# Softmax over rows of 512: interleaving loads and stores in one DMA queue

## The chip, the cores and the metric

The kernel runs on one core of a Trainium2 chip. The metric is the time of one execution on the device, in microseconds. The engines named here are TensorE (PE, not used for arithmetic in this kernel), VectorE (DVE), ScalarE (ACT), GpSimd (POOL) and SyncE (SP), which only issues transfers. "held" is the buffer on the chip; "DRAM" is the memory off the core, where the input and the output lie.

## The reference

The input x has 16 x 1024 x 512 values of float32, so 16384 rows of 512. Each row is replaced by its softmax:

```python
x_max = np.max(x, axis=-1, keepdims=True)
exp_x = np.exp(x - x_max)
return (exp_x / np.sum(exp_x, axis=-1, keepdims=True)).astype(np.float32)
```

33.55 MB are read and 33.55 MB are written.

## The kernel before

**Tiles.** 128 partitions each hold 128 rows. The rows of a partition are counted 0 to 127 and cut into 16 groups of 8 (GROUP), and into 8 blocks of 16 (BLOCKS), so a block is two groups. A block is 128 partitions x 16 rows x 2 KB, 4 MB in all, and is one transfer: one load from x or one store to out. The text calls the loads L0 to L7 and the stores S0 to S7; block n holds groups 2n and 2n+1.

**The buffer.** held has room for 96 rows per partition (RING), so for six blocks. Blocks 0 to 5 have rows of their own. Block 6 uses the rows of block 0 again and block 7 those of block 1, so L6 may start only when S0 has landed, and L7 only when S1 has.

**The work on a group.** DVE takes the negated maximum of each row (step M, L164). ACT runs eight activations, one for each row slot, that write the exponential in place and add up the row's sum (L195); it goes through the groups 0 to 15 in order. DVE takes the reciprocal of the sums (L170). Then the group is multiplied by it in place (L172): on POOL for groups 0 to 11 (step P), on DVE for groups 12 to 15 (step V). The order of DVE's steps is written out by hand in VECTOR: it begins M0 M1 P0 M2 P1 M3 and goes on with M8 P6 M9 P7 and so forth, and ends with

```python
P10 M12 P11 M13 V12 M14 V13 M15 V14 V15
```

Here a P step is the reciprocal on DVE, which releases POOL's multiplication, so DVE's wait for M12's load stands ahead of the reciprocal of group 11.

**The order of transfers.** All transfers are issued by SP, on one hardware queue, in the order of the list ORDER. The first AHEAD entries, all of them loads, are issued without a wait at the start of the program (the first even ahead of the program's start barrier, in loads_at_the_head). The rest follows in a loop: ahead of a load SP waits for the stores that free its rows (semaphore stored), ahead of a store it waits for the scaling of the store's two groups (semaphores scaled):

```python
for what, k in ORDER[AHEAD:]:
    if what == "L":
        ...
        load(k)
    else:
        ...
        nc.sync.dma_start(out=in_dram(out_rows, *k), in_=rows(*k)).then_inc(
```

SP runs its list strictly in order: while it waits for one entry, the next ones stand behind it. Each load has a semaphore of its own that the M step of its first group waits for; at the end SP waits for the stores that no load has waited for. The load's issue is at L126, the store's at L152, and all waits of an engine's queue are at L110.

In the kernel before, ORDER is six loads, three stores, two loads, five stores.

Of the kernel before, what the change touches and what calls it, by code (L numbers as in the profile page):

```python
# [1 line left out]

# [4 lines left out]

F32 = mybir.dt.float32
EXP = mybir.ActivationFunctionType.Exp
AX = mybir.AxisListType.X  # L10

GROUP = 8
GROUPS = 16
RING = 12 * GROUP

BLOCKS = [(0, 16), (16, 32), (32, 48), (48, 64), (64, 80), (80, 96), (96, 112), (112, 128)]
ORDER = [
    ("L", (0, 16)),
    ("L", (16, 32)),
    ("L", (32, 48)),
    ("L", (48, 64)),
    ("L", (64, 80)),
    ("L", (80, 96)),
    ("S", (0, 16)),
    ("S", (16, 32)),  # L30
    ("S", (32, 48)),
    ("L", (96, 112)),
    ("L", (112, 128)),
    ("S", (48, 64)),
    ("S", (64, 80)),
    ("S", (80, 96)),
    ("S", (96, 112)),
    ("S", (112, 128)),
]
AHEAD = 6  # L40

VECTOR = """
    M0 M1 P0 M2 P1 M3 P2 M4 P3 M5 P4 M6 P5 M7 P6 M8 P7 M9 P8 M10 P9 M11
    P10 M12 P11 M13 V12 M14 V13 M15 V14 V15
"""

AT_HEAD = {mybir.EngineType.SP: 1}

def loads_at_the_head(nc):

    main, body = nc.main_func.blocks[0], nc.main_func.blocks[1]
    for engine, count in AT_HEAD.items():
        loads = [
            i
            for i in body.instructions
            if i.engine == engine and type(i).__name__ == "InstDMACopy"  # L60
        ][:count]
        barrier = next(
            n
            for n, i in enumerate(main.instructions)
            if i.engine == engine and type(i).__name__ == "InstDrain"
        )
        for load in loads:
            body.instructions.remove(load)
        main.instructions[barrier:barrier] = loads


@with_exitstack
def kernel(
    ctx: ExitStack,
    tc: tile.TileContext,
    x: bass.AP,
    out: bass.AP,
):
    nc = tc.nc
    nc.at_finalize(loads_at_the_head)  # L80
    P = nc.NUM_PARTITIONS

    d = x.shape[-1]
    x_rows, out_rows = x.flatten_outer_dims(), out.flatten_outer_dims()
    assert x_rows.shape[0] == GROUPS * GROUP * P

    def in_dram(rows, a, b):

        first, last = next(k for k in BLOCKS if k[0] <= a and b <= k[1])
        block = rows[first * P : last * P].rearrange("(p r) d -> p r d", p=P)  # L90
        return block[:, a - first : b - first, :]

    held = nc.alloc_sbuf_tensor("held", [P, RING, d], F32).ap()
    shift = nc.alloc_sbuf_tensor("shift", [P, GROUPS * GROUP], F32).ap()
    sums = nc.alloc_sbuf_tensor("sums", [P, GROUPS * GROUP], F32).ap()
    recip = nc.alloc_sbuf_tensor("recip", [P, GROUPS * GROUP], F32).ap()

    loads = [k for what, k in ORDER if what == "L"]
    stores = [k for what, k in ORDER if what == "S"]
    loaded = {k: nc.alloc_semaphore(f"loaded{k[0]}") for k in loads}  # L100
    scaled = [nc.alloc_semaphore(f"scaled{g}") for g in range(GROUPS)]
    stored = {k: nc.alloc_semaphore(f"stored{k[0]}") for k in stores}
    maxed = nc.alloc_semaphore("maxed")
    expd = nc.alloc_semaphore("expd")
    to_pool = nc.alloc_semaphore("to_pool")
    to_vector = nc.alloc_semaphore("to_vector")

    def take(engine, semaphore, n):

        engine.wait_ge(semaphore, n).then_inc(semaphore, -n)  # L110

    def rows(a, b):
        assert a // RING == (b - 1) // RING
        return held[:, a % RING : (b - 1) % RING + 1, :]

    def meets(k, a, b):
        return k[0] < b and a < k[1]

    def group(g):
        return g * GROUP, (g + 1) * GROUP  # L120

    def stats(t, g):
        return t[:, g * GROUP : (g + 1) * GROUP]

    def load(k):
        copy = nc.sync.dma_start(out=rows(*k), in_=in_dram(x_rows, *k))  # L126
        copy.then_inc(loaded[k], 16)
        return copy

    with tc.manual_schedule():
        for _, k in ORDER[:AHEAD]:
            tc.no_tile_sem_insts.add(load(k).ins.name)
    tc.close()
    tc.compile()  # L137

    taken, done = set(), set()
    for what, k in ORDER[AHEAD:]:  # L140
        if what == "L":
            for s in stores:
                if meets(s, k[0] - RING, k[1] - RING) and s not in taken:
                    take(nc.sync, stored[s], 16)
                    taken.add(s)
            load(k)
        else:
            for g in range(GROUPS):
                if meets(k, *group(g)) and g not in done:
                    take(nc.sync, scaled[g], 1)  # L150
                    done.add(g)
            nc.sync.dma_start(out=in_dram(out_rows, *k), in_=rows(*k)).then_inc(  # L152
                stored[k], 16
            )


    seen = set()

    def rowmax(g):
        for k in loads:  # L160
            if meets(k, *group(g)) and k not in seen:
                take(nc.vector, loaded[k], 16)
                seen.add(k)
        nc.vector.reduce_max(  # L164
            out=stats(shift, g), in_=rows(*group(g)), axis=AX, negate=True
        ).then_inc(maxed, 1)

    def scale(g, engine, ready):
        take(nc.vector, expd, 1)
        nc.vector.reciprocal(out=stats(recip, g), in_=stats(sums, g)).then_inc(ready, 1)  # L170
        take(engine, ready, 1)
        engine.tensor_mul(  # L172
            out=rows(*group(g)),
            in0=rows(*group(g)),
            in1=stats(recip, g).unsqueeze(2).to_broadcast([P, GROUP, d]),
        ).then_inc(scaled[g], 1)

    for step in VECTOR.split():
        what, g = step[0], int(step[1:])
        if what == "M":  # L180
            rowmax(g)
        elif what == "V":
            scale(g, nc.vector, to_vector)
        else:
            scale(g, nc.gpsimd, to_pool)


    nc.scalar.preload_act_table(EXP)  # L188

    with nc.scalar.Fori(0, GROUPS) as i:  # L190
        take(nc.scalar, maxed, 1)
        for r in range(GROUP):
            row = held[:, bass.ds(i % (RING // GROUP) * GROUP + r, 1), :]
            at = bass.ds(i * GROUP + r, 1)
            act = nc.scalar.activation(  # L195
                out=row,
                in_=row,
                func=EXP,
                bias=shift[:, at],
                scale=1.0,  # L200
                accum_out=sums[:, at],
            )
        act.then_inc(expd, 1)


    for k in stores:
        if k not in taken:
            take(nc.sync, stored[k], 16)


# [1 line left out]
_INS = ['x']  # L212
_OUTS = [((16, 1024, 512), 'float32')]


# [23 lines left out]
```

## Time and profile before

| What | Value |
|---|---|
| Median of 3 runs | 160.15 us (160.12 to 160.21) |
| Profiled execution | 160.14 us, of which the span shown is 158.8 us |
| DVE, ACT, POOL busy | 90.6, 92.0 and 84.0 us |
| DMA queue busy | 98.9% of 16 engines' span, 67.11 MB |
| One maximum of a group on DVE (L164) | 4399 ns, 16 of them |
| One exponential on ACT (L195) | 712 ns, 128 of them |
| One scaling on POOL and on DVE (L172) | 7015 ns and 4570 ns |

The busy shares say how long an engine worked in the whole span. The waits say for what an engine stood still. For transfers two numbers are read together: when SP issued one (its start in the timeline), and how long it took from issue to landing; the sum is when the data had arrived. A transfer that is issued while others are still in the queue has their time in its own.

### The profile page before, as it was taken

Reading aid. Unit: us, or ns where it says so; the run is one execution under the profiler, and the core shown is the slowest. Engines: PE = TensorE matmul, PEld = TensorE weight load, DVE = VectorE, ACT = ScalarE, POOL = GpSimd, SP = SyncE. Lnnn points to the kernel's source line nnn. Section 1 sums busy time; section 2 is a strip of 40 time slices with the busy share of each in tenths; the row PEclk is TensorE's granted clock in tenths of the full one; section 3 lists DMA queues with packets and bytes.
Section 4 is the critical chain, followed back from the end, with each engine's and each line's share of the span. In section 5 each row is a group of like instructions: output and inputs, shape, how many; then the busy total and the mean of one; then the engine's idle time right before and its main releaser. Section 6 shows DMA issues by size and latency. Waiting matters only on the chain. (4 is left out here: it accounts for less than half of the span.)

```text
span 158.8 us, 747 instructions
## 1 busy us (share of the span) xinstructions
DVE 90.6 (57%) x36; ACT 92.0 (58%) x257; POOL 84.0 (53%) x16
## 2 busy tenths in 40 slices
DVE  0008959777977977887700000795999998640000
ACT  0300699999999999999993000059934929200000
POOL 0000009999999999999999999259200000000000
DMA  7999999999999998999999999999999999999996
GB/s 264 470 454 396 413 487 421 396 454 470 396 396 487 437 396 380 413 396 454 470 396 421 462 437 396 446 479 396 421 446 454 396 437 473 413 404 454 446 413 264
DMA packets 2305, 67.12 MB, mean 423 GB/s; under 512 B 256, under 2 KB 256, under 8 KB 256
## 3 DMA queue, kind: packets, MB, share of 16 engines
q1 hardware_dynamic: 2304, 67.11, 98.9%
q14 instruction: 1, 0.01, 0.0%
HBM read 33.55 MB, written 33.55 MB: 423 GB/s over the span
## 5 line engine op out<-in xcount | busy, mean ns | idle before, releaser
L195 ACT ACTIVATE held<-held,shift x128 | 90.3, 712 | 40.0 <-ACTq L110 40.0
L172 POOL TENSOR_TENSOR held<-held,recip 128x4096 f32<-128x4096 f32 x12 | 83.8, 7015 | 28.0 <-POOLq L110 28.0
L164 DVE TENSOR_REDUCE shift<-held 128x8 f32<-128x4096 f32 x16 | 70.3, 4399 | 33.2 <-DVEq L110 33.2
L195 ACT ACTIVATION_READ_ACCUMULATOR held<-held,shift x128 | 24.6, 192 | 0.0
L172 DVE TENSOR_TENSOR held<-held,recip 128x4096 f32<-128x4096 f32 x4 | 18.3, 4570 | 0.6
L170 DVE RECIPROCAL recip<-sums 128x8 f32<-128x8 f32 x16 | 3.2, 201 | 16.5 <-DVEq L110 16.5
L188 ACT ACT_TABLE_LOAD x1 | 1.3, 1283 | 3.9 <-PEq L137 3.9
L223 POOL MEMSET const-float32-0.0<- 128x1 f32 x1 | 0.1, 98 | 0.2 <-issue 0.2
L223 POOL MEMSET const-uint8-127<- 128x1 uint8 x1 | 0.1, 102 | 0.0
L223 POOL MEMSET const-bfloat16-1.0<- 128x1 bf16 x1 | 0.1, 101 | 0.0
L223 POOL MEMSET const-float32-1.0<- 128x1 f32 x1 | 0.1, 98 | 0.0
## 6 DMA issues: line engine op xcount, KB each, us to landing
held<-in_x_dram SPq DMA_DIRECT2D x8, 4096.0 KB, 29.7
out_dram<-held SPq DMA_DIRECT2D x8, 4096.0 KB, 28.3
```

The lines of the kernel that those rows point to most:

```text
L164: nc.vector.reduce_max(out=stats(shift, g), in_=rows(*group(g)), axis=AX, negate=True).then_inc(maxed, 1)
L170: nc.vector.reciprocal(out=stats(recip, g), in_=stats(sums, g)).then_inc(ready, 1)
L172: engine.tensor_mul(out=rows(*group(g)), in0=rows(*group(g)), in1=stats(recip, g).unsqueeze(2).to_broadcast([P, GROUP, d]),).then_inc(scal ...
L188: nc.scalar.preload_act_table(EXP)
L195: act = nc.scalar.activation(out=row, in_=row, func=EXP, bias=shift[:, at], scale=1.0, accum_out=sums[:, at],)
L223: nc = _bacc.Bacc("TRN2", target_bir_lowering=False, num_devices=1)
```

## The change

The list ORDER is rewritten and AHEAD goes from 6 to 5. Afterwards SP issues five loads, then S0, L5, S1, L6, S2, L7, and then S3 to S7. Nothing else is edited. In the built program the instructions of DVE, ACT and POOL stand in the same order as before; only SP's list differs. On it, the wait for S0's landing (for L6) now stands ahead of the wait for groups 4 and 5 (for S2), and L5 stands behind the wait for groups 0 and 1 (for S0).

```diff
     ("L", (32, 48)),
     ("L", (48, 64)),
     ("L", (64, 80)),
+    ("S", (0, 16)),
     ("L", (80, 96)),
-    ("S", (0, 16)),
     ("S", (16, 32)),
+    ("L", (96, 112)),
     ("S", (32, 48)),
-    ("L", (96, 112)),
     ("L", (112, 128)),
     ("S", (48, 64)),
     ("S", (64, 80)),
@@ -37,7 +37,7 @@
     ("S", (96, 112)),
     ("S", (112, 128)),
 ]
-AHEAD = 6
+AHEAD = 5
```

## The prediction

> **What bounds the kernel now.** I read the page first: busy times, slices, DMA queues, chain. Columns in the first two parts: busy us and share of the span, then tenths and GB/s in 40 slices of 3.97 us.
>
> ```profile
> DVE 90.6 (57%) x36; ACT 92.0 (58%) x257; POOL 84.0 (53%) x16
> ...
> DMA  7999999999999998999999999999999999999996
> GB/s 264 470 454 396 413 487 421 396 454 470 396 396 487 437 396 380 413 396 454 470 396 421 462 437 396 446 479 396 421 446 454 396 437 473 413 404 454 446 413 264
> ...
> q1 hardware_dynamic: 2304, 67.11, 98.9%
> HBM read 33.55 MB, written 33.55 MB: 423 GB/s over the span
> ...
> DVE held L172 3%
> ```
>
> No compute engine is over 58% busy, while the one DMA queue works for 98.9% of the span and has no empty slice. The chain of waits reaches back only to the last scale (3% of the span): after it comes one long transfer that the chain does not follow.
>
> Next, where each transfer ends. The timeline gives an issue's start (first column), and the DMA view, narrowed to that issue, the time to landing (last column). The fifth load, the sixth, the first store and the last store:
>
> ```profile
> 2.16 0.44 SPq L126 DMA_DIRECT2D held<-in_x_dram  x1
> 2.65 0.49 SPq L126 DMA_DIRECT2D held<-in_x_dram  x1
> 37.54 0.35 SPq L152 DMA_DIRECT2D out_dram<-held  x1
> 140.91 0.33 SPq L152 DMA_DIRECT2D out_dram<-held  x1
> ```
>
> ```profile
> held<-in_x_dram SPq DMA_DIRECT2D x1, 4096.0 KB, 48.9
> held<-in_x_dram SPq DMA_DIRECT2D x1, 4096.0 KB, 58.8
> out_dram<-held SPq DMA_DIRECT2D x1, 4096.0 KB, 33.6
> out_dram<-held SPq DMA_DIRECT2D x1, 4096.0 KB, 17.9
> ```
>
> Issue plus time to landing: the fifth load (call it L4, counting from 0) lands at 2.16 + 48.9 = 51.1, L5 at 61.5, store S0 at 71.1, S7 at 158.8, which is the span's end. The same sum for the others gives L0 12.2, L1 21.9, L2 31.6, L3 41.3; S1 80.9, S2 90.8, L6 100.3, L7 110.1; S3 119.8, S4 129.6, S5 139.4, S6 149.1. So transfers land one by one in the order of issue, 9.7 to 9.8 us apart whether they load or store. Only L5, the last before the first turn from loads to stores, takes 10.4: 0.7 more. The turn from stores to loads (S2 to L6: 9.5, rounded) and the second turn from loads to stores (L7 to S3: 9.7) show nothing.
>
> Last, what the compute engines wait for:
>
> ```profile
> 68.27 4.42 DVE L164 TENSOR_REDUCE shift<-held 128x8 f32<-128x4096 f32 x1
> 73.89 4.37 DVE L164 TENSOR_REDUCE shift<-held 128x8 f32<-128x4096 f32 x1
> 79.41 0.20 DVE L170 RECIPROCAL recip<-sums 128x8 f32<-128x8 f32 x1 [1.16 <-DVEq L110]
> 100.45 4.42 DVE L164 TENSOR_REDUCE shift<-held 128x8 f32<-128x4096 f32 x1 [20.83 <-DVEq L110]
> 136.38 4.43 DVE L172 TENSOR_TENSOR held<-held,recip 128x4096 f32<-128x4096 f32 x1
> ```
>
> The maxima M10 and M11 (first two lines) use L5 about 7 us after it landed. M12 stands still for 20.83 us until L6 lands at 100.3. The last scale ends at 140.8, but S6 holds the queue until 149.1, so even the last store waits 8.2 us behind other transfers.
>
> **The change, part by part.** The bytes, the sixteen transfers, their sizes and all compute instructions stay; only SP's list changes. New queue order: L0 to L4, S0 L5 S1 L6 S2 L7, S3 to S7.
>
> *Five loads at the head instead of six.* L0 to L4 are issued and land as before, the last at 51.1. S0 is issued when POOL has scaled groups 0 and 1, as now at 37.5, which is 13.6 us before the queue would run dry (now 24). L5 needs no store to have landed (it takes free rows), so it follows S0 at about 37.9. One issue of 0.49 us leaves the head; nothing waits for it, since the DVE's first work waits for L0 at 12.2.
>
> *S0 ahead of L5.* They exchange places: S0 lands near 61.5, L5 at 71.1, together the same 20.0 us that the two take now. L5 is 9.6 us later, and M10 goes from 68.27 to about 71.3: 3 us late on the DVE. ACT finishes exp 9 at 73.8 and then waits for M10 until 75.7; exps 10 and 11 (8 rows at 0.705, 5.64 us each) end at 81.3 and 87. POOL runs P0 to P10 without a break to 100.2 (P9 at 86.2, P10 at 93.2). Recip 9, behind M10, is done by 75.9, recip 10 by 81.5: 10 and 11 us of cover. Without this cover each further us would pass to S4 and S5, which still have over 20 us of slack below.
>
> *S1 ahead of L6, L6 ahead of S2.* S1 is issued at 51.5 as now (its groups), while the queue is full until 71.1. L6 needs S0's rows: SP waits for S0's landing and issues L6 at 61.6 instead of 71.28. Behind this wait in SP's queue stands S2, whose groups are ready at 65.4, so it loses nothing. L6 lands at 90.8, 9.5 earlier; S2 at 100.3.
>
> *L7 behind S2.* It needs S1, and SP waits till 80.9, as now (80.96). Behind it stands S3, ready at 79.5 by POOL and issued at about 81.4; now 81.48. L7 lands at 110.1, as now.
>
> *What follows.* M12 starts at 90.9 rather than 100.45 and the DVE's 20.83 us hole mostly closes. P11 starts at 100.2 instead of 105.16 and ends at 107.2: S5 at 107.3 (112.27 now). V12 runs from about 101.3; in the trace its kind took 5.00 us where it shared 0.7 us with a POOL scale, otherwise 4.43. Now it lies wholly beside P11. Lower bound 5.0, upper bound: it waits for P11's end, 107.2 + 4.4 = 111.6. I take the upper one. Then M14 (L7 landed at 110.1) ends at 116.0, and V13, M15, V14, V15, each with a 0.2 us reciprocal and short gaps, at 120.8, 125.2, 129.9 and 135.5. S6 is issued at 120.9 (125.56 now), S7 at 135.6 (140.91).
>
> *The sum.* The queue is filled until, at each issue: S1 71.1 (20 ahead), L6 80.9 (19), S2 90.8 (25), L7 100.3 (19), S3 110.1 (29), S4 at 93.3 119.8 (26), S5 129.6 (22), S6 139.4 (18), S7 149.1 (13). Thus no transfer is ever awaited by the queue; the earlier compute of 5 us buys slack for S7 and no time. The end stays at 12.2 + 15 places x 9.73 + 0.7 of one turn = 158.8. The profiled execution took 160.14 with a span of 158.8, so 1.3 us lie outside; the median before is 160.15. Forecast: 160.15.
>
> *The unknown: turns.* The order has three changes of direction now and seven afterwards; from load to store two now, four afterwards. One turn, the first, shows 0.7 us; the two others show none within the rounding. Bounds for the four added turns: 0 and 4 x 0.7 = 2.8; below nothing at most the 0.7 itself. I take 0, by the nearest rows, the later turns, which like the new ones stand in a queue already writing; the first turn stays, in another place.
>
> The Trainium skill, "DMA: Bandwidth & Descriptors", section "Anatomy of one DMA — SWDGE (gpsimd) path", gives a DMA a nearly constant cost of about 2.0 us, mostly the confirmation of the last written bytes; paid again at four added turns that would be +8, an estimate from that page. By the trace here it is not paid between queued transfers: 9.7 us apart, whatever the direction.
>
> **The rivals.**
>
> *Slower: every turn from load to store stalls the queue.* Place: the last packets of a load before a store. Price: 0.7 per turn, as at L5. Two turns are added: 160.15 + 1.4 = 161.5; with only one of them, 160.8. It decides from 0.16 us a turn (two make the 0.32 of the bound below). For: L5's landing. Against: L7 to S3, 9.7. Chance 0.20. That all four turns cost 0.7 (162.9): 0.03.
>
> *Slower: a full drain at each turn.* As a mechanism of this kernel it is the queue standing empty between two directions; a load alone at the head shows that: L0 lands 12.2 after issue instead of 9.7, so 2.5 a turn and 4 x 2.5 = 10: 170. Against: three turns in the trace at 0.7 or less. Chance 0.02. The skill's fixed cost named above is such a rule.
>
> *Slower: the later L5 becomes the bound.* It would need S4 over 26 us late; chance 0.02, 161 or more.
>
> *Faster: the 0.7 belongs to six loads in a row, not to the first store.* Then five loads escape it: 160.15 - 0.7 = 159.45. For: the excess is in a load's time, and L0 to L4 have none. Against: it comes right at the first store. More is hardly to be had: the other places are at 9.7 already, and loads and stores take the same, so mixing has nothing to overlap. Chance 0.15.
>
> *Not doing what it says:* the built order of SP is the one described, so no chance for that.
>
> **The numbers.** Runs of before lie within 0.1 us; a difference of 0.2% (0.32 us) is about what a measurement of this kernel can tell from no change. No change 0.58; slower 0.20 + 0.03 + 0.02 + 0.02 = 0.27; faster 0.15. The range takes in the loss of the one stall below, 159.4, and two turns above, 161.6; it leaves out about 1 in 10. The likeliest case alone spans 159.9 to 160.4.
>
> **What would show it.** Right: the DMA row full in every slice at 98.9%; landings near 61.5 (S0), 71.1 (L5), 90.8 (L6), 110.1 (L7), 158.8 (S7); M10 near 71.3, M12 near 90.9, the last scale ending near 135, S7 landing over 20 us after its issue. Wrong: places of more than 9.8 us at S0, S1, S2 or S3 (a price per turn); a landing of S0 9.7 after L4 (the stall is gone); a slice of the DMA row below 9 in the middle (starved queue); or a scale that ends after the store ahead of it has landed.

## The result and the profile after

The kernel after takes 160.78 us in the median of 13 runs (160.28 to 162.16), the kernel before 160.12 in 13 runs beside them. The ratio is 1.0042, 95% interval 1.0026 to 1.0058: slower by 0.67 us (0.42 to 0.93). Its runs also lie further apart than those of before (160.05 to 161.10). The profiled execution took 160.39 us with a span of 159.1, so it shows a little over a third of the loss (160.39 against 160.14). No slower run of after has a trace; what the rest of the loss consists of is inferred from the traces of the other kernels below.

The page of after, busy times, slices and queue:

```profile
DVE 94.8 (60%) x36; ACT 92.1 (58%) x257; POOL 83.9 (53%) x16
...
DMA  7999999999999999999999999999999999999996
GB/s 264 478 445 396 437 486 396 396 478 445 396 445 346 396 445 461 412 396 461 461 396 420 445 445 404 445 461 404 429 437 445 414 429 437 445 420 437 453 412 264
...
q1 hardware_dynamic: 2304, 67.11, 98.9%
```

The queue is still full from end to end, with the same 98.9%. Apart from the two ends, the lowest slice, 346 GB/s, is now the 13th (47.7 to 51.7 us), where L4 turns into S0; in before the dip (380) was the 16th, at L5 and S0. Nothing ran dry, yet the same bytes took longer.

The timeline of SP and the DMA view of after for L4, S0, L5, L6 and S7 (issue first, time to landing last):

```profile
2.18 0.44 SPq L126 DMA_DIRECT2D held<-in_x_dram  x1
37.45 0.35 SPq L152 DMA_DIRECT2D out_dram<-held  x1
37.85 0.43 SPq L126 DMA_DIRECT2D held<-in_x_dram  x1
61.92 0.33 SPq L126 DMA_DIRECT2D held<-in_x_dram  x1
135.83 0.33 SPq L152 DMA_DIRECT2D out_dram<-held  x1
```

```profile
held<-in_x_dram SPq DMA_DIRECT2D x1, 4096.0 KB, 49.7
out_dram<-held SPq DMA_DIRECT2D x1, 4096.0 KB, 24.4
held<-in_x_dram SPq DMA_DIRECT2D x1, 4096.0 KB, 33.5
held<-in_x_dram SPq DMA_DIRECT2D x1, 4096.0 KB, 29.1
out_dram<-held SPq DMA_DIRECT2D x1, 4096.0 KB, 23.2
```

L4 lands at 51.9 (51.1 before), S0 at 61.9, L5 at 71.4, L6 at 91.0, S7 at 159.0. S7 stands 23.2 us in the queue. The compute engines have no part in the end. DVE's timeline of after, M10, M12, V12 and V15:

```profile
71.52 4.42 DVE L164 TENSOR_REDUCE shift<-held 128x8 f32<-128x4096 f32 x1 [3.27 <-DVEq L110]
91.12 4.42 DVE L164 TENSOR_REDUCE shift<-held 128x8 f32<-128x4096 f32 x1 [8.73 <-DVEq L110]
102.12 9.25 DVE L172 TENSOR_TENSOR held<-held,recip 128x4096 f32<-128x4096 f32 x1
131.31 4.42 DVE L172 TENSOR_TENSOR held<-held,recip 128x4096 f32<-128x4096 f32 x1
```

M10 is 3.3 us late and M12 9.3 us early, as worked out; the last scale ends at 135.7.

**Where the time is.** A transfer is cut into 128 packets of 32 KB, eight for each of 16 DMA engines. The trace has a record of each packet, and about nine in ten of them, loads and stores alike, take 1213 ns. The records do not name the engine; the packets fall into 16 chains, as each starts within a few ns of another's end, and a chain is taken for an engine. What a packet takes beyond 1213 ns (beyond 611 ns, for one of 16 KB) is called excess here. Summed over an engine's packets and averaged over the 16 engines, for the two profiled executions:

```
                                        before   after
start of L0                              0.64    0.59 us
load ahead of the first store (L5, L4)   0.90    0.99
after only: L5 ahead of S1                -      0.08
after only: L6 ahead of S2                -      0.09
L7 ahead of S3                           0.01    0.09
everything else                          0.07    0.07
mean excess of an engine                 1.62    1.91
the slowest engine's end behind the mean 0.49    0.61
```

The later excess sits in the last packet or two of a load that is followed by a store; no store that is followed by a load has it. The mean engine loses 0.29 us more. The slowest engine, which alone ends the last store, is 0.12 further behind the mean, but this difference by itself shows nothing: in traces of other kernels with the two turns of before it is 0.49 to 0.78 behind (E1 0.78, E3 0.75, E7 0.49), and in before it comes from a single halt of one engine in S5 (0.30 us without a packet, and the next one 0.38 us longer). In after it comes from the turns: the engine that ends last is 0.27 us behind the mean when L4 ends, 0.36 after L5, 0.48 after L6, 0.67 after L7, and hardly moves during the stores (0.61 at the end).

### The profile page after: what moved, and what is told of

Same layout as the page of the kernel before. It is cut to its first block, busy times and chain, and to the rows that moved or that the text cites. A ratio compares the mean times of both kernels' runs of the same rounds, so it can differ in the third digit from the quotient of the medians.

```text
span 159.1 us, 747 instructions
## 1 busy us (share of the span) xinstructions
DVE 94.8 (60%) x36; ACT 92.1 (58%) x257; POOL 83.9 (53%) x16
## 3 DMA queue, kind: packets, MB, share of 16 engines
q1 hardware_dynamic: 2304, 67.11, 98.9%
## 5 line engine op out<-in xcount | busy, mean ns | idle before, releaser
L195 ACT ACTIVATION_READ_ACCUMULATOR held<-held,shift x128 | 24.0, 187 | 0.0
L172 DVE TENSOR_TENSOR held<-held,recip 128x4096 f32<-128x4096 f32 x4 | 22.5, 5632 | 0.6
```

The costliest lines, as they stand in the source:

```text
L172: engine.tensor_mul(out=rows(*group(g)), in0=rows(*group(g)), in1=stats(recip, g).unsqueeze(2).to_broadcast([P, GROUP, d]),).then_inc(scal ...
L195: act = nc.scalar.activation(out=row, in_=row, func=EXP, bias=shift[:, at], scale=1.0, accum_out=sums[:, at],)
```

## The experiments

Theory A is that each turn from load to store costs time in the DMA engines; B, that five loads instead of six ahead of the first store do. Changes in us are the ratio to before, in runs beside each other, times 160.15, with the 95% interval. The ratio is not that of the two medians; where they tell different things, both are given.

**E1, the head alone.** Edit: `-AHEAD = 6` to `+AHEAD = 5`, the order of before kept.

> The order of before, but only five loads issued at the head (AHEAD 5); L5 is then issued a little later, still without a wait, and still ahead of S0. Theory A (each load followed by a store costs time at the turn; two turns here as before): 160.1. Theory B (what costs is that five instead of six loads run ahead of the first store): 160.1, since the queue's order is unchanged. If the later issue of L5 itself were the cause: about 160.8, as after.

Measured: 160.24, ratio 0.9996 (0.9986 to 1.0005). The later issue of L5 costs nothing.

**E2, one more turn.**

```diff
     ("L", (64, 80)),
+    ("S", (0, 16)),
     ("L", (80, 96)),
-    ("S", (0, 16)),
     ("S", (16, 32)),
...
-AHEAD = 6
+AHEAD = 5
```

> Five loads, S0, L5, S1, S2, L6, L7, then the five last stores: three turns from load to store, one more than before. Theory A: after added two turns and 0.66 us, so a third of a us each: 160.45. Theory B (five loads ahead of the first store): all of it, 160.8.

Measured: 160.42, ratio 1.0019 (1.0002 to 1.0036), so +0.30 (0.03 to 0.58); the medians differ by 0.16. The added turn, L5 to S1, has a mean excess of 0.10 us, and up to 0.39 on one engine.

**E3, five loads, but two turns as before.**

```diff
     ("L", (64, 80)),
-    ("L", (80, 96)),
     ("S", (0, 16)),
     ("S", (16, 32)),
     ("S", (32, 48)),
+    ("L", (80, 96)),
     ("L", (96, 112)),
...
-AHEAD = 6
+AHEAD = 5
```

> Five loads, S0 S1 S2, L5 L6 L7, then the five last stores: two turns from load to store, as before, but five loads at the head. L5 lands near 91, so M10 is late; by the trace's durations the last scale still ends near 142, ahead of the queue. Theory A: 160.1. Theory B: 160.8.

Measured: 160.31, ratio 1.0004 (0.9995 to 1.0012). Theory B falls: five loads ahead of the first store cost nothing while the turns stay at two.

**E4, five turns.** ORDER is L0 to L3, S0 L4 S1 L5 S2 L6 S3 L7, S4 to S7, and AHEAD 4.

> Four loads, then S0 L4 S1 L5 S2 L6 S3 L7, then the four last stores: five turns from load to store, three more than before. Theory A: 160.1 + 3 x 0.33 = 161.1. Theory B (the shorter the run of loads ahead of the first store, the more): two fewer loads, 161.4; the two differ in e3, here only a price below 160.5 would speak against both.

Measured: 162.08, ratio 1.0106 (1.0071 to 1.0141), so +1.70 (1.14 to 2.26), more than three times a third of a us and more than either theory said. By issue plus time to landing, the loads L4 to L7 ahead of a store take 10.0, 10.0, 10.1 and 10.2 us from the landing before them, and the stores 9.7. The end of the queue shows how that comes about. The windows view (length, busy time of DVE, ACT and POOL, clock, DMA share, GB/s of the packets that start in the window), first before, then this kernel:

```profile
157.00:157.50 0.50, 0.00 (x0) 0.00 (x0) 0.00 (x0) 1.00 0.31 131
157.50:158.00 0.50, 0.00 (x0) 0.00 (x0) 0.00 (x0) 1.00 0.01 0
158.00:158.50 0.50, 0.00 (x0) 0.00 (x0) 0.00 (x0) 1.00 0.00 0
```

```profile
157.00:157.50 0.50, 0.00 (x0) 0.00 (x0) 0.00 (x0) 1.00 0.46 197
157.50:158.00 0.50, 0.00 (x0) 0.00 (x0) 0.00 (x0) 1.00 0.16 66
158.00:158.50 0.50, 0.00 (x0) 0.00 (x0) 0.00 (x0) 1.00 0.31 131
```

131 GB/s for 0.5 us are two packets of 32 KB. Before, the last two engines start their last packet before 157.5; here three packets start after that, two of them after 158, while the other engines have nothing left to do. The mean engine ends only 0.10 us later than in before (157.91 against 157.82); the slowest, at 159.57, is 1.66 behind the mean instead of 0.49. It was 0.61 behind when L3 ended, then 0.68, 0.88, 1.31 and 1.72 after L4, L5, L6 and L7.

**E5 and E6, a small store early.** Edit on before and on after, AHEAD 2 in both; not shown: POOL fills the tile warm with zeros at the start, and SP waits for warm_done ahead of S0.

```diff
     ("L", (16, 32)),
+    ("W", None),
     ("L", (32, 48)),
...
+        elif what == "W":
+            take(nc.sync, warmed, 1)
+            nc.sync.dma_start(
+                out=in_dram(out_rows, 127, 128)[:, :, 0:128], in_=warm
+            ).then_inc(warm_done, 16)
```

> The order of before with one small extra store (128 x 512 bytes of zeros into rows of out that S7 writes over later) behind L1, so that a store has gone out long before S0. Theory F (the stall of about 0.9 us at the end of L5 is paid once, at the first store of the program): the stall moves to L1 or vanishes, and the packets of L5 show none; 160.1 if it moves, 159.3 if a small store pays less. Theory T (a stall at the turn after a long run of loads, whatever was stored before): L5 shows its 0.9 again, and the extra turn adds 0.1 to 0.9: 160.3 to 161.1.

> The order of after with the same small extra store behind L1. Theory F: L4 shows no stall, the later turns keep their small ones: 160.0 to 160.8. Theory T: L4 shows 0.9 again, 160.9 to 161.7.

Measured: 160.34 (ratio 1.0004, 0.9992 to 1.0016) and 160.68 (1.0022, 1.0002 to 1.0042). The stall ahead of S0 is still there, 0.85 us on L5 and 0.86 on L4, so a small store ahead does not pay it; theory F falls for a store of 64 KB. The time of E6 lies below the 160.9 that theory T said. The store itself takes 0.19 us of the queue and its turn shows no more than that. The two kernels differ by 0.34 in the medians, half of what before and after differ by.

**E7 and E8, before and after without most of the arithmetic.**

```diff
-            out=stats(shift, g), in_=rows(*group(g)), axis=AX, negate=True
+            out=stats(shift, g), in_=rows(*group(g))[:, :, 0:16], axis=AX, negate=True
...
-            row = held[:, bass.ds(i % (RING // GROUP) * GROUP + r, 1), :]
+            row = held[:, bass.ds(i % (RING // GROUP) * GROUP + r, 1), 0:16]
```

and so for the scale.

> The order of before; maxima, exponentials and scales work on 16 of the 512 columns only (most of the arithmetic is left out), the transfers are whole. The DMA queue is full either way. Theory A (turns cost in the DMA engines themselves): 160.1, with a 0.9 us stall at L5. Rival C (what costs at the turns is the compute engines' traffic on held): the stall is gone, 159.2.

> The order of after with the same thin compute. Theory A: 160.8, so 0.66 above e7. Rival C, or a cause in the later L5 or in the scales that stand beside each other: the same as e7 within 0.1.

The pages of the two, busy times and DMA row:

```profile
DVE 7.3 (5%) x36; ACT 39.3 (25%) x257; POOL 5.0 (3%) x16
...
DMA  7999999999999998999999999999999999999996
```

```profile
DVE 7.3 (5%) x36; ACT 39.3 (25%) x257; POOL 5.0 (3%) x16
...
DMA  7999999999999999999999999999999999999994
```

Measured: 160.03 (ratio 0.9985, 0.9973 to 0.9996) and 160.65 (1.0031, 1.0016 to 1.0046). With DVE at 5% and POOL at 3% the order of after still costs 0.62 us in the medians, and the first stall is there too (0.86 and 0.91). Rival C falls; the later M10 and the scale that stands beside another have no part in it. E7 itself is 0.24 us below before (0.06 to 0.43); its trace does not show why (mean excess 1.59 against 1.62).

**E9, six loads at the head and one turn added late.**

```diff
     ("L", (96, 112)),
+    ("S", (48, 64)),
     ("L", (112, 128)),
-    ("S", (48, 64)),
     ("S", (64, 80)),
```

> The order of before with six loads at the head, and S3 moved between L6 and L7: three turns from load to store instead of two, nothing else. Theory A (a turn after a single load costs 0.1 to 0.3 us, partly by putting the 16 engines further out of step): 160.3 to 160.5, with an excess on the last packets of L6 and L7 before the stores. Theory B (the head of five loads): 160.1. By the trace's durations the last scale ends near 146, still ahead of S7's place at 149; if that failed, the queue would show a gap ahead of S7.

Measured: 160.37, ratio 1.0035 (1.0005 to 1.0064), so +0.56 (0.08 to 1.02). Three of its twelve runs, from 161.81 to 162.21, carry most of this; the medians differ by 0.18, and one of the 24 runs of before beside it took 161.81 too. DVE's last scale and the DMA row of this kernel:

```profile
140.44 4.42 DVE L172 TENSOR_TENSOR held<-held,recip 128x4096 f32<-128x4096 f32 x1
```

```profile
DMA  7999999999999999999999999999999999999994
```

The scale ends at 144.9, ahead of S7's place, and no slice is short of work until the last. L6 ahead of S3 has a mean excess of 0.07 and L7 ahead of S4 0.16; the stall of 0.86 at L5 is that of before. So a turn costs with six loads at the head as well, though this run shows it barely clear of the noise.

**E10 and E11, halved transfers, few turns and many.** Edit: BLOCKS of 8 rows. E10 (AHEAD 12): L0 to L11, S0 to S5, L12 to L15, S6 to S15. E11 (AHEAD 10): L0 to L9, then S0 L10 S1 L11 to S5 L15, then S6 to S15.

> All transfers halved (16 loads and 16 stores of 2 MB, 8 rows per partition), in the order of before: twelve loads, six stores, four loads, ten stores, so two turns from load to store. It is the control for the next kernel. Theory A: 160.1 to 160.4 (twice as many transfers, none of them turning).

> Halved transfers in the order of after: ten loads, then S0 L10 S1 L11 and so on to L15, then ten stores: seven turns from load to store, five more than the control. Theory A with a price per turn: 5 x 0.33 = 1.7 above the control, more if the engines get further out of step with each turn (three added turns cost 1.8 in the run of four loads). Rival: the price goes with the bytes that alternate, then 0.7 above the control, as after is above before.

Measured: 160.75 (ratio 1.0038, 1.0026 to 1.0051) and 162.72 (1.0160, 1.0141 to 1.0178). E10 missed its expectation: halving costs 0.61 us by itself, its steady places being 4.862 us for 2 MB, so 9.72 for two against 9.68 for one of 4 MB. E11 is 1.97 above E10 in the medians: five turns of 0.39, though only half as many bytes alternate in each. The price goes with the turns. The mean engine ends about 0.6 us later than in E10, and the slowest is 1.9 behind the mean instead of 0.5. The windows of E11's end:

```profile
158.50:159.00 0.50, 0.00 (x0) 0.00 (x0) 0.00 (x0) 1.00 0.23 98
159.00:159.50 0.50, 0.00 (x0) 0.00 (x0) 0.00 (x0) 1.00 0.15 66
159.50:160.00 0.50, 0.00 (x0) 0.00 (x0) 0.00 (x0) 1.00 0.08 33
160.00:160.50 0.50, 0.00 (x0) 0.00 (x0) 0.00 (x0) 1.00 0.08 33
```

For the last 1.5 us one to four packets of 16 KB start in each half microsecond: a few late engines hold the end.

**E12 to E14, the transfers at the first turn halved.** In E10 the last load ahead of the first store has 0.11 us of mean excess instead of 0.90. Edits on before: L5 as two loads (E12), S0 as two stores (E13), both (E14, shown); AHEAD is 7 where L5 is halved:

```diff
-    ("L", (80, 96)),
-    ("S", (0, 16)),
+    ("L", (80, 88)),
+    ("L", (88, 96)),
+    ("S", (0, 8)),
+    ("S", (8, 16)),
```

> The order of before, with L5 as two loads of 2 MB (8 rows each). In the kernel with all transfers halved the turn behind the first run of loads took 0.11 us in the mean of the engines instead of 0.9. Theory P (the first turn's stall belongs to large packets of 32 KB in the load): the stall shrinks to 0.1 to 0.3 and the time to about 159.5. Rival Q (it belongs to the store that follows, or to anything else): the stall stays, 160.2.

> The order of before, with S0 as two stores of 2 MB. Theory P: the stall stays, 160.2. Rival Q (it belongs to the large packets of the first store): it shrinks, 159.5.

> The order of before, with both L5 and S0 as two transfers of 2 MB. Under P or Q: 159.5, as the better of the two; if the stall needs both sides small: 159.5 only here; if only halving everything removes it (as a slower pace of all loads, which that kernel also had): 160.2 in all three.

Measured: 160.20, 160.28 and 160.26, ratios 0.9994 (0.9983 to 1.0005), 1.0011 (1.0002 to 1.0020) and 1.0007 (0.9998 to 1.0016). The stall stays, at about 0.8, 0.8 and 0.5 us in the mean. P and Q both miss, and the times are those of the third case, 160.2 in all three. But the stall of E14 is smaller than the others without a gain in time. In E10 the six loads ahead of the turn were each up to 0.03 slower as well; what makes the stall small there is not found. No version faster than before came out of this.

## Why the prediction was wrong

The forecast was no change, with 0.58; the time is 0.67 us slower, inside the range and on the side that had 0.27.

**The step that failed** is "The unknown: turns", where the price of an added turn was taken as 0 by the nearest rows. It measured 0.2 to 0.6 us: two added turns 0.67, one 0.30 (E2) and 0.56 (E9), or 0.16 and 0.18 in the medians, three 1.70 (E4), none -0.06 and 0.06 (E1, E3); five added turns of half-size transfers 1.97. The bounds, 0 to 0.7 a turn, held it. The rival "every turn from load to store stalls the queue" named the right place, the last packets of a load before a store, and was mis-sized at 0.7; its threshold of 0.16 a turn was passed.

**Why the row misled.** The turn from L7 to S3 in before, 9.7 from landing to landing, was read as free, and in that execution it was (0.01 mean excess). It is not a fixed price, though: in E13 and E14, whose full-size loads and stores have the order of before, the same turn shows 0.15 and 0.08, in E1, E3 and E7 0.01. In the traces of after, E2, E4, E6, E8 and E9, at 17 later turns, the four engines that start the last packet of a load earliest have a mean excess of 0.04 us on it, and the four that start it latest 0.19. Whoever is behind loses more, so the 16 engines drift apart from turn to turn, and the last store ends with the slowest: 0.49 to 0.78 us behind the mean in before, E1, E3 and E7, 0.61 to 1.09 with one or two added turns (after, E2, E6, E8, E9), 1.66 with three (E4). The prediction's sum has no such term: it gives each transfer one place in the queue, as if the 16 engines were one. Growth faster than the number of turns (E4) agrees with the drift; the five added turns of E11, 0.39 each, do not show such growth. That the drift also makes the spread between runs was not tested.

The drift is not the whole of it. At L7 in before, E1, E3 and E7 the engines start the last packet 0.5 to 0.8 us apart and the mean excess is 0.01; at L5 in after they are 0.56 apart and it is 0.08. Each added turn of these experiments stands behind a single load, the turn at L7 in those four behind two or three. So the price may also depend on how many loads run ahead of the turn; no run adds a turn behind two loads, and this stays open.

**The first turn's stall.** Right: it stays and moves to the store's new place (0.90 on L5, 0.99 on L4). The rival in which five loads escape it, 159.45, did not happen. E3 shows it with five loads too (0.82), E7 without compute. What causes it stays open: not the number of loads from five up (after four, in E4, it is 0.45), not the arithmetic, not the lack of a small store before, not the size of either transfer beside it alone. With both halved it is 0.5 and with all halved 0.1, so the size has a part in it that is not understood.

**Cover and waits** were right within 0.5 us, apart from L4, which landed at 51.9 and not at 51.1 as before: the stall sits on the load ahead of the first store. S0 61.9 (61.5 said), L5 71.4 (71.1), L6 91.0 (90.8), M10 71.52 (71.3), M12 91.12 (90.9), the last scale's end 135.7 (135.5), S7 135.83 to 159.0 (135.6 to 158.8). The sign named for a price per turn, places of more than 9.8 us at S0 to S3, showed at S0 and S1 (9.9 each) and not at S2 and S3 (9.8 each); it is a weak sign, since S2 took 9.9 in before as well. V12, for which the upper bound was taken, ended at 111.4 (111.6).

**The full drain at each turn**, 2.5 us, is refuted by E4: three added turns cost 1.70. The Trainium skill, "DMA: Bandwidth & Descriptors", section "Anatomy of one DMA — SWDGE (gpsimd) path", has a nearly fixed cost of about 2.0 us for each DMA on the path that it describes, that of transfers issued by GpSimd. No run here uses that path; in the full queue of this kernel, issued by SP, neither a transfer nor a turn pays that, as transfers land 9.7 us apart and a turn costs some 0.2 to 0.6.

## What to carry to other kernels

In a kernel bound by one full DMA queue, keep loads and stores in long runs: each added change from load to store, behind a single load, cost 0.2 to 0.6 us here, although the queue never ran dry and no wait appeared. A transfer ends with the slowest of its 16 engines, so look at the tail of the queue in windows of half a microsecond and not at the mean rate alone. One free event in a profile is a weak price for several of them; if its cost can depend on the state that earlier ones leave, the forecast should lie inside the bounds and not on one.

## What was not expected of the hardware

Loads and stores both took 1213 ns for about nine in ten packets of 32 KB, 27.0 GB/s an engine, whether the kernel computes fully or hardly at all (89% of the packets in before, 90% in E7). Interleaving the directions gained nothing and cost some. V12 took 9.25 us instead of 4.43 beside a POOL scale: POOL's twelve scales ran from 23.36 to 107.09 without a break, and V12 ended at 111.37, 4.28 after them. In before, where V12 took 5.00, it ended 4.28 after POOL's last scale as well (116.45 and 112.17). The Trainium skill, "SBUF — State Buffer", section "SBUF: two separate sides", says that a VectorE instruction with two inputs in SBUF, the memory on the chip that holds these buffers, and a GpSimd instruction that reads SBUF take one shared port pair as an exclusive lock, and that the later one blocks entirely; the trace agrees, as V12 ends about one scale's time after POOL's last.
